# RWKV-7 and MLA trunk layer on one core: a new order for the first FFN's start, for the small RWKV weights and for the first chunk of head group 1

## The chip, the cores and the metric

One core of a Trainium2 chip runs the whole layer. The metric is device time in microseconds (us) of one execution, taken as the median of three runs. Traces come from one further, profiled execution.

## The reference, cut to what matters

T = 256 tokens, width 2048, FFN width 5504, one layer, all in f32.

```
x += 0.5 * post(FFN1(pre(x)))                 FFN = (silu(h @ w_gate) * (h @ w_up)) @ w_down
x += post((g_A * MLA(h) + g_B * RWKV7(h)) @ w_o),   h = pre(x)
x += post(XAttn(pre(x), mem))                 256 memory tokens, 4 heads
x += 0.5 * post(FFN2(pre(x)))

RWKV7, 16 heads of 64, per token t and head:
  w, a, g    from low-rank products (tanh(dw) @ w_w2, da @ w_a2, sigmoid(dg) @ w_g2)
  sa = S a_t;   S = S * w_t + sa (kk*a)_t + v_t k_t;   o_t = S r_t
  o = group_norm(o) * lnx_w + lnx_b + bonus;   y = (o * g) @ w_ob
```

pre and post are RMS norms; g_A and g_B are sigmoids of h times a gate weight of 2 x 2048 columns.

## The kernel before, in words

**Products.** Every weight is split into a high part that the TensorE's fast f32 mode keeps exactly (`whi`) and the rest (`wlo`), and every activation too (`hT` holds both). A weight tile of 128x1024 goes by the SP queue into one of four `wraw` buffers (L177), ACT casts it to `whi` (L179), DVE subtracts to get `wlo` (L180); three such pairs of slots exist. `lin_ch` makes outputs with channels on partitions: per k two matmuls for each 128 columns, L201 with `whi` (512 wide, both parts of the activation) and L204 with `wlo` (256 wide). `lin_tok` makes outputs with tokens on partitions: three matmuls of 512 (L222, L223, L224) per k and token half, and these three are called a step here; a gate chunk of 512 columns has 32 steps. `weights` issues the loads and splits ahead of use, so DVE and ACT do splits among their other work, each engine in one fixed order.

**Order.** A scheduler orders every engine's instructions by a priority that the program sets (`priority`, `hot`, `ahead`), and `after` adds a dependency by hand. On the chip each engine runs its list in order.

**First FFN.** x comes transposed (xT), times the norm's gain, straight into `hT` in pieces (`feed`), and the norm's row of 1/rms is applied to the products afterwards: the sums of squares come from x itself (`X`, four loads of 512 KB), `rstd` is finished by POOL's pow, and `row` spreads it over the partitions with two matmuls (`rB`, L264). The first gate and up columns (c0 = 0) are run in turns of four k.

**RWKV part.** Heads come in two groups of eight (g = 0, 1). `rw_prep` makes the low-rank products from the small weights `ww` (w_w2 and w_a2, matmul `lora`, L727), decay scans and so on; `rw_gram` makes 32x32 blocks of products per chunk of 32 tokens in `G`; `rw_inverse` writes the blocks to DRAM, inverts them row by row on DVE (`TT`, `tm`), writes the result to DRAM (`td`) and loads it back into `G` with four loads. `rw_chain` then runs eight chunks in sequence: `pu` (L875, needs `G`), the copy `uv` on DVE (L876), `pn` (L880) and `po`. After a chunk POOL's queue writes the output (`osc`). `rw_group_norm` loads them again (`ov`), normalises on DVE with a pow on POOL (`gv`), multiplies by g (`pg`) and transposes into `zh` and `zl` for w_ob.

Because chain and inverse leave TensorE idle, matmuls of other products fill it: the first product of the mixers' output (`out_a`, w_oa) and the eight gate chunks (`gate`, steps of three matmuls, called gates 0 to 7 here), whose results go to `ya` or by POOL's queue to `t1d`.

Of the kernel before, what the change touches and what calls it, by code (L numbers as in the profile page):

```python
# [10 lines left out]
F32 = mybir.dt.float32  # L11
# [3 lines left out]
ALU = mybir.AluOpType  # L15
# [12 lines left out]
RING = 3  # L28
STILL = (64, 32)
SKEW = 4  # L30
LEAD = 100
# [46 lines left out]
class Layer:  # L78
    def __init__(self, ctx, tc, a):
# [112 lines left out]

    def lin_ch_steps(self, w, nk, c0, n, x, evac, feed=None):

        nc = self.nc
        nt = n // P
        ps = [self.psm.tile([P, 2, T], F32, tag="mm", name="mm") for _ in range(nt)]
        for k, hi, lo in self.weights(w, nk, c0, n, feed, True):
            for j in range(nt):
                s = slice(j * P, (j + 1) * P)  # L200
                both = lambda: nc.tensor.matmul(ps[j], hi[:, s], x[:, k], start=(k == 0), stop=(k == nk - 1))  # L201
                if k < nk - 1:
                    both()
                nc.tensor.matmul(ps[j][:, 0, :], lo[:, s], x[:, k, 0], start=False, stop=False)  # L204
                if k == nk - 1:
                    both()
            yield k
        for j in range(nt):
            y = self.tmp.tile([P, T], F32, tag="half", name="half", bufs=2)
            nc.scalar.copy(out=y, in_=ps[j][:, 1, :])  # L210
            nc.vector.tensor_add(y, y, ps[j][:, 0, :])  # L211
            evac(j, y)

    def lin_tok(self, w, nk, c0, n, xh, xl, evac, skew=0):
# [5 lines left out]
        def step(t, k, hi, lo):  # L220
            s = slice(t * P, (t + 1) * P)
            nc.tensor.matmul(ps[t], xh[:, k, s], hi, start=(k == 0), stop=False)  # L222
            nc.tensor.matmul(ps[t], xh[:, k, s], lo, start=False, stop=False)  # L223
# [34 lines left out]

    def row(self, r):

        nc = self.nc
        ps = self.pss.tile([P, T], F32, tag="sm", name="rB")
        for t in range(NT):
            nc.tensor.matmul(  # L264
                ps[:, t * P : (t + 1) * P], r[t].broadcast_to([P, P]), self.ident, start=True, stop=True)
        out = self.stat.tile([P, T], F32, tag="row", name="row", bufs=2)
        nc.scalar.copy(out=out, in_=ps)
        return out

    def lazy_row(self, r):  # L270
        made = []

        def get():
            if not made:
                made.append(self.row(r() if callable(r) else r))
            return made[0]

        return get
# [64 lines left out]
    def pre_norm_input(self, srcT, gain, pool):  # L343
# [61 lines left out]
    def ffn(self, normed, wg, wu, wd, post):  # L405
        nc = self.nc
        h, _, row, *feed = normed
        with self.tc.tile_pool(name="hid", bufs=1) as hid:
            mh = hid.tile([P, KF, T], F32R, tag="mh", name="mh")
            ml = hid.tile([P, KF, T], F32R, tag="ml", name="ml")  # L410
            for c0 in range(0, DFF, 256):
                n = min(256, DFF - c0)
                gate = {}
# [12 lines left out]

                if c0 == 0:
                    both = (self.lin_ch_steps(wg, KD, c0, n, h, ev_gate, *feed),
                            self.lin_ch_steps(wu, KD, c0, n, h, ev_up))
                    for k in range(0, KD + 4, 4):  # L430
                        for steps in both:
                            for _ in zip(range(4), steps):
                                pass
                    continue
                self.lin_ch(wg, KD, c0, n, h, ev_gate)
                self.lin_ch(wu, KD, c0, n, h, ev_up)
            return self.post_norm(
# [263 lines left out]
    def rw_alloc(self, pool):  # L701
        self.pad(pool, 32)
        self.ar = pool.tile([P, NC, GP, P], F32, tag="ar", name="ar")
        self.bk = pool.tile([P, NC, GP, P], F32, tag="bk", name="bk")
        self.uv = pool.tile([P, NC, GP, 64], F32, tag="uv", name="uv")
        self.osc = self.dram.tile([T, 1024], F32, name="osc")
        self.nc.gpsimd.memset(self.ar, 0.0)

    def rw_prep(self, pool, g, r, k, bon):
        nc, a = self.nc, self.a  # L710
        p4 = lambda nm: pool.tile([P, GP, T], F32, tag="p4", name=nm, bufs=6)
        ww = pool.tile([P, 512], F32, tag="ww", name="ww")
        cs = slice(g * 512, (g + 1) * 512)
        nc.gpsimd.dma_start(out=ww[:64], in_=a["w_w2"][:, cs])
        nc.gpsimd.dma_start(out=ww[64:], in_=a["w_a2"][:, cs])
        for h in range(2):
# [109 lines left out]
    def rw_inverse(self, pool, G):  # L826
# [26 lines left out]
        for b in range(0, nb, nb // 2):  # L853
            for h in range(2):
                q = slice(h * C, (h + 1) * C)
                bs = slice(b, b + nb // 2)
                nc.sync.dma_start(out=gv[q, bs, q], in_=td[h, bs].rearrange("b s t -> s b t"))

    def rw_chain(self, pool, g, G, wc):
        nc = self.nc  # L860
        S = None
        for c in range(NC):
# [11 lines left out]
            for p in range(GP):  # L874
                nc.tensor.matmul(pu[:, p, :], G[:64, c, p, :64], rhs[:, p, :], start=True, stop=True)  # L875
            nc.vector.tensor_copy(out=self.uv[:64, c], in_=pu)  # L876
# [81 lines left out]
    def mix(self, normed, xsp, stop=None):  # L958
# [3 lines left out]
        with tc.tile_pool(name="mixp", bufs=1) as mp:  # L962
# [15 lines left out]
            with tc.tile_pool(name="rwkv", bufs=1) as pool:  # L978
# [8 lines left out]
                for g in range(2):  # L987
# [5 lines left out]
                    with self.hot():  # L993
                        self.rw_gram(G)
                        self.rw_inverse(pool, G)
                        self.rw_chain(pool, g, G, wc)
                    last_o.append(self.last_o)
                with self.priority(B + 10000):
                    for c in range(8):
                        s = slice(c % 4 * 512, (c % 4 + 1) * 512)  # L1000

                        def use0(t, x):
                            nc.vector.scalar_tensor_tensor(
                                out=ya[:, t, s], in0=x, scalar=1.0, in1=ya[:, t, s], op0=ALU.add, op1=ALU.mult)

                        def use1(t, x):
                            nc.gpsimd.dma_start(out=t1d[t * P : (t + 1) * P, s], in_=x)

                        self.gate(mp, normed, c, use0 if c < 4 else use1)
                tc.cur_priority = E  # L1010
# [115 lines left out]
def layer(ctx: ExitStack, tc, a, stop=None):  # L1126
    L = Layer(ctx, tc, a)

    def block(t, c):
        if c % 2 == 0:  # L1130
            s = slice(c * 512, (c + 2) * 512)
            load = tc.nc.sync.dma_start(out=L.X[:, t, s], in_=a["x"][t * P : (t + 1) * P, s])
            L.after(load, L.last_split)
        return L.X[:, t, c * 512 : (c + 1) * 512]

    h, feed = L.pre_norm_input(a["xT"], "n_ffn1_pre", L.hpool)
    normed = (h, *L.input_stats(block), feed)
    update = L.ffn(normed, a["w_ffn1_gate"], a["w_ffn1_up"], a["w_ffn1_down"], a["n_ffn1_post"])
# [85 lines left out]
```

## Time and profile before

| | |
|---|---|
| median of three runs | 2405.56 us (2404.24 to 2406.37) |
| profiled execution | 2409.81 us, span 2408.0 us, granted clock 0.993 |
| PE, DVE, ACT, POOL busy | 98%, 62%, 48%, 4% of the span |
| DMA | 450 MB, mean 187 GB/s |
| first FFN starts its matmuls at | 4.54 us |
| inverse, group 0 / group 1, ends | 1062.2 / 1233.6 us |
| chain, group 0 / group 1, first pu | 1071.8 / 1244.95 us |

A row of a timeline has start, duration, engine, line, operation, output<-inputs, shape and count, and in brackets the idle time before it with what ended it. A row of a window has the stretch, its length, the busy time (with count) of PE, weight load, DVE, ACT and POOL, the granted TensorE clock (1.00 is full), the DMA engines' busy share and GB/s. A row of waits names the waiting instruction, the one waited for, and total, number and longest of the waits in us. SPq and POOLq are the DMA queues of these engines.

### The profile page before, as it was taken

Reading aid. Unit: us, or ns where it says so; the run is one execution under the profiler, and the core shown is the slowest. Engines: PE = TensorE matmul, PEld = TensorE weight load, DVE = VectorE, ACT = ScalarE, POOL = GpSimd, SP = SyncE. Lnnn points to the kernel's source line nnn. Section 1 sums busy time; section 2 is a strip of 40 time slices with the busy share of each in tenths; the row PEclk is TensorE's granted clock in tenths of the full one; section 3 lists DMA queues with packets and bytes.
Section 4 is the critical chain, followed back from the end, with each engine's and each line's share of the span. In section 5 each row is a group of like instructions: output and inputs, shape, how many; then the busy total and the mean of one; then the engine's idle time right before and its main releaser. Section 6 shows DMA issues by size and latency. Waiting matters only on the chain.

```text
span 2408.0 us, 33178 instructions
## 1 busy us (share of the span) xinstructions
PE 2353.1 (98%) x12666; PEld 2005.5 (83%) x12666; DVE 1487.1 (62%) x2262; ACT 1145.0 (48%) x1703; POOL 87.8 (4%) x132
## 2 busy tenths in 40 slices
PE   8999999999999999999999999999999999999997
PEld 6888888888887887888877688987888888888886
DVE  5666666654447576785874756556766666664444
ACT  6544444444346555443433446545645444544443
POOL 0000000000000102002012100000000000000000
PEclk9999999999999999999999999999999999999999
DMA  7555555556666654463664666545555555566654
GB/s 253 188 191 193 188 189 192 190 191 195 198 199 198 214 175 132 148 190 109 191 196 137 235 230 206 171 155 167 185 192 191 188 190 193 188 198 195 201 194 144
DMA packets 138719, 450.23 MB, mean 187 GB/s; under 512 B 24000, under 2 KB 26560, under 8 KB 138304
## 3 DMA queue, kind: packets, MB, share of 16 engines
q1 hardware_dynamic: 132896, 434.17, 55.8%
q0 software_dynamic: 4944, 13.64, 1.9%
q8 instruction: 99, 1.62, 0.3%
q10 hardware_dynamic: 720, 0.30, 0.1%
q14 instruction: 60, 0.49, 0.1%
HBM read 437.56 MB, written 10.49 MB: 186 GB/s over the span
## 4 chain that ended last, share of the span: by engine, by line
PE 91%; DVE 3%; DMA 3%; issue 2%; ACT 1%; POOL 1%; SPq 0%; DVEq 0%; POOLq 0%; ACTq 0%
PE mm L201 31%; PE mm L204 16%; PE mm L223 13%; PE mm L224 13%; PE mm L222 13%; DVE wlo L180 1%; PE gr L821 1%; DVE X L400 1%; PE pn L880 1%; ACT whi L179 1%; PE po L866 1%; DMA ov<-osc 0%; PE po L889 0%; PE po L868 0%; PE pu L875 0%
## 5 line engine op out<-in xcount | busy, mean ns | idle before, releaser
L180 DVE TENSOR_TENSOR wlo<-wraw,whi 128x1024 fp32r<-128x1024 f32 (+2 forms) x796 | 958.2, 1206 | 709.2 <-ACT whi L179 696.9
L179 ACT CAST whi<-wraw 128x1024 fp32r<-128x1024 f32 (+2 forms) x796 | 824.0, 1037 | 895.3 <-PE mm L224 470.2
L201 PE MATMUL mm<-hT,whi 128*128 128x512 f32 x3296 | 1147.9, 394 | 6.6 <-DVE hT L292 5.4
L204 PE MATMUL mm<-hT,wlo 128*128 128x256 f32 x3296 | 913.5, 283 | 2.1 <-DVE wlo L180 2.1
L201 PEld LDWEIGHTS mm<-hT,whi 128*128 128x128 f32 x3296 | 614.1, 188 | 134.3 <-ACT whi L179 6.9
L204 PEld LDWEIGHTS mm<-hT,wlo 128*128 128x128 f32 x3296 | 621.5, 189 | 13.1 <-DVE wlo L180 4.1
L222 PE MATMUL mm<-whi,mh 128*128 128x512 f32 x688 | 267.6, 389 | 1.2 <-ACT whi L179 1.2
L223 PE MATMUL mm<-wlo,mh 128*128 128x512 f32 x688 | 267.8, 389 | 0.5 <-DVE wlo L180 0.5
L224 PE MATMUL mm<-whi,ml 128*128 128x512 f32 x688 | 267.7, 389 | 0.0
L223 PE MATMUL mm<-wlo,hT 128*128 128x512 f32 (+2 forms) x512 | 189.0, 369 | 3.5 <-DVE wlo L180 3.4
L222 PE MATMUL mm<-whi,hT 128*128 128x512 f32 (+2 forms) x512 | 187.1, 367 | 2.0 <-ACT whi L179 1.6
L224 PE MATMUL mm<-whi,hT 128*128 128x512 f32 (+2 forms) x512 | 187.8, 367 | 0.0
L222 PEld LDWEIGHTS mm<-whi,mh 128*128 128x128 f32 x688 | 129.1, 188 | 28.1 <-ACT whi L179 1.5
L223 PEld LDWEIGHTS mm<-wlo,mh 128*128 128x128 f32 x688 | 129.1, 188 | 27.7 <-DVE wlo L180 1.0
L224 PEld LDWEIGHTS mm<-whi,ml 128*128 128x128 f32 x688 | 129.2, 188 | 26.9
L210 ACT COPY half<-mm 128x256 f32<-128x256 f32 x206 | 75.1, 366 | 136.8 <-PE mm L201 136.8
L211 DVE TENSOR_TENSOR half<-half,mm 128x256 f32<-128x256 f32 x206 | 85.7, 418 | 53.0 <-ACT half L210 53.0
L223 PEld LDWEIGHTS mm<-wlo,hT 128*128 128x128 f32 x512 | 97.9, 191 | 19.8 <-DVE wlo L180 5.7
L222 PEld LDWEIGHTS mm<-whi,hT 128*128 128x128 f32 x512 | 97.8, 192 | 16.4 <-ACT whi L179 2.3
L224 PEld LDWEIGHTS mm<-whi,hT 128*128 128x128 f32 x512 | 97.9, 191 | 13.7 <-issue 0.2
L256 POOL TENSOR_TENSOR rstd<-rstd,mhalf 128x1 f32<-128x1 f32 x22 | 12.1, 553 | 1809.8 <-DVE rstd L254 1809.8
L222 PE MATMUL mm<-whi,oT 128*128 128x512 f32 x128 | 51.1, 401 | 1.4 <-ACT whi L179 1.4
(279 smaller groups left out, 1857.6 us busy)
## 6 DMA issues: line engine op xcount, KB each, us to landing
wraw<-in_w_ffn_up SPq DMA_DIRECT2D x172, 512.0 KB, 3.3
wraw<-in_w_ffn_gate SPq DMA_DIRECT2D x171, 512.0 KB, 3.3
wraw<-in_w_ffn_down SPq DMA_DIRECT2D x168, 512.0 KB, 4.2
wraw<-in_w_in SPq DMA_DIRECT2D x124, 512.0 KB, 3.5
wraw<-in_w_o SPq DMA_DIRECT2D x32, 512.0 KB, 4.3
wraw<-in_w_ckv SPq DMA_DIRECT2D x31, 512.0 KB, 3.5
wraw<-in_w_oa SPq DMA_DIRECT2D x16, 512.0 KB, 3.4
wraw<-in_w_ob SPq DMA_DIRECT2D x16, 512.0 KB, 4.8
```

Source lines behind the costliest of these rows:

```text
L179: cast = nc.scalar.copy(out=hi[:, e], in_=raw[:, e])
L180: self.last_split = nc.vector.tensor_sub(out=lo[:, e], in0=raw[:, e], in1=hi[:, e].bitcast(F32))
L201: both = lambda: nc.tensor.matmul(ps[j], hi[:, s], x[:, k], start=(k == 0), stop=(k == nk - 1))
L204: nc.tensor.matmul(ps[j][:, 0, :], lo[:, s], x[:, k, 0], start=False, stop=False)
L210: nc.scalar.copy(out=y, in_=ps[j][:, 1, :])
L211: nc.vector.tensor_add(y, y, ps[j][:, 0, :])
L222: nc.tensor.matmul(ps[t], xh[:, k, s], hi, start=(k == 0), stop=False)
L223: nc.tensor.matmul(ps[t], xh[:, k, s], lo, start=False, stop=False)
L224: self.last_mm = nc.tensor.matmul(ps[t], xl[:, k, s], hi, start=False, stop=(k == nk - 1))
L400: return nc.vector.scalar_tensor_tensor(out=x, in0=y[:, t, s], scalar=r[t], in1=x, op0=ALU.mult, op1=ALU.add)
L821: nc.tensor.matmul(ps[:, p, :], self.bk[:, c, p, :], self.ar[:, c, p, :], start=True, stop=True)
L866: nc.tensor.matmul(po[:, p, :], self.ar[:, c, p, :], S[:, p, :], start=(p == 0), stop=False)
```

## The change

Five edits:

- In the first FFN the four k of an xT tile share one `wraw` buffer (`self.xraw`); each of the four loads of x is issued after one four-k turn's split, in place of all four after the turns; the second gate chunk (c0 = 256) is run right behind them, into PSUM buffers of the tag "tr" (`spare`), and `rB` is tied behind its last matmul (`last_ch`).
- `rw_small` makes `ww` the first tile of the RWKV pool, with its loads ahead of the memset of `ar`.
- The gates are written ahead of group 1's chain.
- Group 1's first `pu` is tied behind the last matmul of gate step 210 (`filler[FIRST_U]`).
- The four loads of `G` go in turn to SP and POOL.

```diff
+FIRST_U = 209
...
-    def lin_ch_steps(self, w, nk, c0, n, x, evac, feed=None):
+    def lin_ch_steps(self, w, nk, c0, n, x, evac, feed=None, spare=False):
-        ps = [self.psm.tile([P, 2, T], F32, tag="mm", name="mm") for _ in range(nt)]
+        pool, tag = (self.pst, "tr") if spare else (self.psm, "mm")
+        ps = [pool.tile([P, 2, T], F32, tag=tag, name="mm") for _ in range(nt)]
...
-                    both()
+                    self.last_ch = both()
...
             self.last_mm = nc.tensor.matmul(ps[t], xl[:, k, s], hi, start=False, stop=(k == nk - 1))
+            self.filler.append(self.last_mm)
...
-    def row(self, r):
+    def row(self, r, prev=None):
...
+            if prev is not None:
+                self.after(one, prev)
...
-                made.append(self.row(r() if callable(r) else r))
+                made.append(self.row(r(), self.last_ch) if callable(r) else self.row(r))
...
         def feed(k0, m):
-            raw = self.wraw.tile([P, 4, T], F32, tag="wraw", name="wraw")
-            nc.sync.dma_start(out=raw[:, :m, :], in_=srcT[:, k0 : k0 + m, :])
+            if k0 % 4 == 0:
+                self.xraw = self.wraw.tile([P, 4, T], F32, tag="wraw", name="wraw")
+            raw = self.xraw[:, k0 % 4 : k0 % 4 + m, :]
+            nc.sync.dma_start(out=raw, in_=srcT[:, k0 : k0 + m, :])
...
+                both = (self.lin_ch_steps(wg, KD, c0, n, h, ev_gate, *feed[:1]),
+                        self.lin_ch_steps(wu, KD, c0, n, h, ev_up))
+                for k in range(0, KD, 4):
+                    for steps in both:
+                        for _ in zip(range(4), steps):
+                            pass
+                    if feed:
+                        feed[1](k // 4)
+                if feed:
+                    ev_gate, ev_up = evacs(256)
+                    third = self.lin_ch_steps(wg, KD, 256, n, h, ev_gate, spare=True)
+                    for _ in zip(range(KD), third):
+                        pass
+                    both = (*both, third)
...
     def rw_alloc(self, pool):
         self.pad(pool, 32)
+        self.rw_small(pool, 0)
...
+    def rw_small(self, pool, g):
+
+        self.ww = pool.tile([P, 512], F32, tag="ww", name="ww")
+        for q, n in ((slice(0, 64), "w_w2"), (slice(64, P), "w_a2")):
+            self.nc.gpsimd.dma_start(out=self.ww[q], in_=self.a[n][:, g * 512 : (g + 1) * 512])
...
-                nc.sync.dma_start(out=gv[q, bs, q], in_=td[h, bs].rearrange("b s t -> s b t"))
+                queue = (nc.sync, nc.gpsimd)[h]
+                queue.dma_start(out=gv[q, bs, q], in_=td[h, bs].rearrange("b s t -> s b t"))
...
+                if c == 0 and behind is not None:
+                    self.after(one, behind)
...
+                    if g == 1:
+                        self.filler = []
+                        with self.priority(B + 10000):
+                            for c in range(8):
...
+                                self.gate(mp, normed, c, use0 if c < 4 else use1)
+                    with self.hot():
+                        self.rw_chain(pool, g, G, wc, self.filler[FIRST_U] if g == 1 else None)
...
+    def load(i):
+        t, s = i // 2, slice(i % 2 * 1024, (i % 2 + 1) * 1024)
+        L.after(tc.nc.sync.dma_start(out=L.X[:, t, s], in_=a["x"][t * P : (t + 1) * P, s]), L.last_split)
```

What the instruction lists show at three places (numbers behind names are buffer numbers; the lines of the changed program differ from those of the profile: L204 and L208 there are L201 and L204 before, L226 to L228 are L222 to L224, L182 is L180, L912 is L875, L915 is L876, L919 is L880).

TensorE in the first FFN, before: the two matmuls of rB inside the second gate chunk (mm_398 and mm_399), the first of them at this place.

```order
L204 MATMUL mm_399<-hT_108,wlo_106 128x256
L201 MATMUL mm_398<-hT_108,whi_104 128x512
L204 MATMUL mm_398<-hT_108,wlo_106 128x256
L201 MATMUL mm_399<-hT_108,whi_104 128x512
L264 MATMUL rB_371<-ident_90,rstd_360 128x128
L204 MATMUL mm_399<-hT_108,wlo_106 128x256
L201 MATMUL mm_398<-hT_108,whi_104 128x512
```

TensorE in the first FFN, after: the end of the second gate chunk (mm_334 and mm_335), rB, and the second up chunk (mm_491 and mm_492).

```order
L204 MATMUL mm_334<-hT_108,whi_104 128x512
L208 MATMUL mm_335<-hT_108,wlo_106 128x256
L204 MATMUL mm_335<-hT_108,whi_104 128x512
L269 MATMUL rB_450<-ident_90,rstd_439 128x128
L269 MATMUL rB_450<-ident_90,rstd_445 128x128
L204 MATMUL mm_491<-hT_108,whi_104 128x512
L208 MATMUL mm_491<-hT_108,wlo_106 128x256
```

rB has moved from inside that chunk to behind its 32 pairs.

TensorE at the start of the RWKV part, before: the last matmuls of the k columns (mm_7698), then sixteen of w_oa (mm_7804 and mm_7805), of which the last five are shown, then lora.

```order
L224 MATMUL mm_7805<-whi_104,oT_7108 128x512
L222 MATMUL mm_7804<-whi_104,oT_7108 128x512
L223 MATMUL mm_7804<-wlo_106,oT_7108 128x512
L224 MATMUL mm_7804<-whi_104,oT_7108 128x512
L222 MATMUL mm_7805<-whi_104,oT_7108 128x512
L727 MATMUL lora_8086<-twa_6274,ww_8077 128x512
L727 MATMUL lora_8090<-twa_6274,ww_8077 128x512
```

After, at the same place:

```order
L204 MATMUL mm_7695<-hT_5731,whi_104 128x512
L226 MATMUL mm_7804<-whi_104,oT_7105 128x512
L226 MATMUL mm_7805<-whi_104,oT_7105 128x512
L762 MATMUL lora_8083<-twa_6271,ww_7796 128x512
L762 MATMUL lora_8087<-twa_6271,ww_7796 128x512
L227 MATMUL mm_7804<-wlo_106,oT_7105 128x512
```

lora has moved ahead of fourteen matmuls of w_oa; on POOL the two loads of ww now stand ahead of the memset of ar instead of behind it.

DVE around the first uv of group 1, before (wlo by the tile of its wraw: 10456 holds k = 6 and 7 of gate 6, 10472 k = 8 and 9).

```order
L919 TENSOR_REDUCE gm_10723<-ov_10719 128x8
L929 TENSOR_TENSOR ov_10691<-ov_10691,gv_10696 128x512
L180 TENSOR_TENSOR wlo_106<-wraw_10456,whi_104 128x1024
L930 TENSOR_TENSOR ov_10691<-ov_10691,lnx_10688 128x512
L920 TENSOR_SCALAR gm_10723<-gm_10723 128x8
L927 TENSOR_TENSOR ov_10719<-ov_10719,bon_7797 128x512
L931 TENSOR_TENSOR ov_10691<-ov_10691 128x512
L180 TENSOR_TENSOR wlo_106<-wraw_10472,whi_104 128x1024
L921 TENSOR_TENSOR ov_10719<-ov_10719,gm_10723 128x512
L876 COPY uv_7801<-pu_9328 64x256
```

After (wraw_10210 holds k = 6 and 7, 10226 k = 8 and 9); the first reduce, of ov_10716, stands eight rows ahead of the first row shown, the low of 10210 six and that of 10226 one.

```order
L969 TENSOR_TENSOR ov_10688<-ov_10688,lnx_10685 128x512
L962 TENSOR_REDUCE gv_10721<-gsc_10719 128x8
L182 TENSOR_TENSOR wlo_106<-wraw_10242,whi_104 128x1024
L970 TENSOR_TENSOR ov_10688<-ov_10688 128x512
L963 TENSOR_SCALAR gv_10721<-gv_10721 128x8
L968 TENSOR_TENSOR ov_10716<-ov_10716,gv_10721 128x512
L182 TENSOR_TENSOR wlo_106<-wraw_10258,whi_104 128x1024
L915 COPY uv_7801<-pu_10445 64x256
```

Between the group norm's first reduce and uv there now stand four lows instead of two, and a product with gv, which POOL's pow makes. On TensorE the first pu stood behind 11 steps and one matmul of gate 6, and now stands behind 18 steps, twenty matmuls later; five matmuls stand between pu and pn in both.

More of the change, by code (lines that the diff above doesn't have):

```diff
@@ L200, in lin_ch_steps @@
                 s = slice(j * P, (j + 1) * P)
-                both = lambda: nc.tensor.matmul(ps[j], hi[:, s], x[:, k], start=(k == 0), stop=(k == nk - 1))
+                both = lambda: nc.tensor.matmul(
+                    ps[j], hi[:, s], x[:, k], start=(k == 0), stop=(k == nk - 1))
                 if k < nk - 1:
@@ L263, in row @@
         for t in range(NT):
-            nc.tensor.matmul(
+            one = nc.tensor.matmul(
                 ps[:, t * P : (t + 1) * P], r[t].broadcast_to([P, P]), self.ident, start=True, stop=True)
+            if prev is not None:
+                self.after(one, prev)
         out = self.stat.tile([P, T], F32, tag="row", name="row", bufs=2)
@@ L410, in ffn, with evacs @@
             ml = hid.tile([P, KF, T], F32R, tag="ml", name="ml")
-            for c0 in range(0, DFF, 256):
-                n = min(256, DFF - c0)
+            def evacs(c0):
                 gate = {}
@@ L425, in ev_up @@
                     self.split(gate[j], mh[:, k, :], ml[:, k, :])
[L427 to L433, printed above, removed]
-                    continue
-                self.lin_ch(wg, KD, c0, n, h, ev_gate)
-                self.lin_ch(wu, KD, c0, n, h, ev_up)
+                return ev_gate, ev_up
+            for c0 in range(0, DFF, 256):
+                n = min(256, DFF - c0)
+                if feed and c0 == 256:
+                    continue
+                ev_gate, ev_up = evacs(c0)
+                if c0:
+                    self.lin_ch(wg, KD, c0, n, h, ev_gate)
+                    self.lin_ch(wu, KD, c0, n, h, ev_up)
+                    continue
+                both = (self.lin_ch_steps(wg, KD, c0, n, h, ev_gate, *feed[:1]),
[12 more added lines that the diff above has]
+                    both = (*both, third)
+                for steps in both:
+                    for _ in steps:
+                        pass
+                if feed:
+                    self.lin_ch(wu, KD, 256, n, h, ev_up)
             return self.post_norm(
@@ L711, in rw_prep @@
         p4 = lambda nm: pool.tile([P, GP, T], F32, tag="p4", name=nm, bufs=6)
[L712 to L715, printed above, removed]
+        if g:
+            self.rw_small(pool, g)
+        ww = self.ww
         for h in range(2):
@@ L874, in rw_chain @@
             for p in range(GP):
-                nc.tensor.matmul(pu[:, p, :], G[:64, c, p, :64], rhs[:, p, :], start=True, stop=True)
+                one = nc.tensor.matmul(pu[:, p, :], G[:64, c, p, :64], rhs[:, p, :], start=True, stop=True)
+                if c == 0 and behind is not None:
+                    self.after(one, behind)
             nc.vector.tensor_copy(out=self.uv[:64, c], in_=pu)
@@ L995, in mix, with use0, use1 @@
                         self.rw_inverse(pool, G)
-                        self.rw_chain(pool, g, G, wc)
-                    last_o.append(self.last_o)
[L998 to L1009, printed above, removed]
+                    if g == 1:
+                        self.filler = []
+                        with self.priority(B + 10000):
+                            for c in range(8):
+                                s = slice(c % 4 * 512, (c % 4 + 1) * 512)
+                                def use0(t, x):
+                                    nc.vector.scalar_tensor_tensor(
+                                        out=ya[:, t, s], in0=x, scalar=1.0, in1=ya[:, t, s], op0=ALU.add, op1=ALU.mult)
+                                def use1(t, x):
+                                    nc.gpsimd.dma_start(out=t1d[t * P : (t + 1) * P, s], in_=x)
+                                self.gate(mp, normed, c, use0 if c < 4 else use1)
+                    with self.hot():
+                        self.rw_chain(pool, g, G, wc, self.filler[FIRST_U] if g == 1 else None)
+                    last_o.append(self.last_o)
                 tc.cur_priority = E
@@ L1127, in layer @@
     L = Layer(ctx, tc, a)
+    def load(i):
+        t, s = i // 2, slice(i % 2 * 1024, (i % 2 + 1) * 1024)
+        L.after(tc.nc.sync.dma_start(out=L.X[:, t, s], in_=a["x"][t * P : (t + 1) * P, s]), L.last_split)
     def block(t, c):
[L1130 to L1133, printed above, removed]
         return L.X[:, t, c * 512 : (c + 1) * 512]
     h, feed = L.pre_norm_input(a["xT"], "n_ffn1_pre", L.hpool)
-    normed = (h, *L.input_stats(block), feed)
+    normed = (h, *L.input_stats(block), feed, load)
     update = L.ffn(normed, a["w_ffn1_gate"], a["w_ffn1_up"], a["w_ffn1_down"], a["n_ffn1_post"])
```

2 lines of the change are left out of this document (1 added, 1 removed).

## The prediction

> **What bounds the kernel now.** I read the page's first lines, then ten-microsecond windows of the start and the middle, then the TensorE's waits there and, around each, the timeline of the engine that is waited for.
>
> ```profile
> span 2408.0 us, 33178 instructions
> PE 2353.1 (98%) x12666; PEld 2005.5 (83%) x12666; DVE 1487.1 (62%) x2262; ACT 1145.0 (48%) x1703; POOL 87.8 (4%) x132
> ```
>
> TensorE is busy in 98% of the span, and the change takes no sizeable work from it. What can be won lies in the 55 us in which it isn't busy and in the stretches where its clock is lower. The parts of the change aim at three of these stretches: the first 50 us, the start of the RWKV part at 935 to 945, and the first chunk of head group 1 at 1241 to 1257.
>
> ```profile
> 10.00:20.00 10.00, 7.79 (x40) 5.93 (x40) 6.89 (x12) 7.39 (x12) 0.00 (x0) 1.00 0.90 289
> 20.00:30.00 10.00, 10.00 (x59) 8.72 (x59) 7.13 (x9) 5.91 (x9) 0.00 (x0) 1.00 0.88 290
> 30.00:40.00 10.00, 6.35 (x37) 5.32 (x35) 4.10 (x8) 6.45 (x15) 0.55 (x1) 1.00 0.94 351
> 40.00:50.00 10.00, 10.00 (x50) 8.82 (x51) 6.01 (x14) 7.77 (x16) 0.55 (x1) 0.83 0.55 193
> ...
> 940.00:950.00 10.00, 7.60 (x26) 4.38 (x25) 1.92 (x2) 6.56 (x14) 3.45 (x4) 1.00 0.71 202
> 1245.00:1302.00 57.00, 55.59 (x389) 45.70 (x390) 26.31 (x43) 15.55 (x26) 9.85 (x17) 0.91 0.35 109
> ```
>
> The columns are busy time of PE, weight load, DVE, ACT and POOL, then the granted clock, the DMA share and GB/s. Between 30 and 40 us TensorE stands for 3.65 us, and from 40 to 50 the clock is 0.83.
>
> **Part 1, the first FFN's start.**
>
> ```profile
> 28.41 1.83 SPq L1132 DMA_DIRECT2D X<-in_x  x4
> 34.90 0.63 ACT L283 ACTIVATE junk<-X 128x512 f32<-128x512 f32 x1 [3.42 <-DMA X<-in_x]
> 40.98 0.63 ACT L283 ACTIVATE junk<-X 128x512 f32<-128x512 f32 x1
> 39.90 0.49 PE L264 MATMUL rB<-ident,rstd 128*128 128x128 f32 x2 [3.65 <-POOL rstd L256]
> 42.76 0.63 PE L201 MATMUL mm<-hT,whi 128*128 128x512 f32 x1
> 43.40 0.63 PE L201 MATMUL mm<-hT,whi 128*128 128x512 f32 x1
> 45.97 0.39 PE L201 MATMUL mm<-hT,whi 128*128 128x512 f32 x1
> 46.32 0.40 PE L201 MATMUL mm<-hT,whi 128*128 128x512 f32 x1
> X<-in_x SPq DMA_DIRECT2D x4, 512.0 KB, 7.7
> ```
>
> The four x pieces go out only at 28.41, each takes 7.7 us to land, the eight sums of squares run from 34.90 to 41.6, and the broadcast of rstd (rB), which stands inside the second gate chunk, makes TensorE wait 3.65 us. After it five pairs come 0.64 us apart instead of 0.35: 5 x 0.29 = 1.45 us. The new order sends one x piece after each four-k stage and puts the whole second gate chunk ahead of rB: 32 pairs x 0.35 = 11.2 us. The last x piece stands behind that chunk's second weight tile on SP; landing (7.7), two sums of squares (1.5) and the rstd steps (about 2) are 11.2 us from its issue, and the issue comes some microseconds before that chunk begins, so I expect no wait at rB: 3.65 + 1.45 = 5.1 us won.
>
> Against it: the x pieces now travel in the four stages in which the DMAs already carry 289 GB/s at a share of 0.90. Three pieces of 512 KB at the 351 GB/s of the third window cost 4.5 us of transfer; the idle tenth of three stages of 5.6 us (16 pairs) holds 1.9, so up to 2.6 us may appear as waits. In return the first xT pieces no longer take a weight buffer each, and up to the 2.2 us that TensorE misses between 10 and 20 can be had. I take these two against each other: -5 us, with ends -7.3 (5.1 + 2.2) and -2.5 (5.1 - 2.6).
>
> The second gate chunk accumulates in the PSUM buffers of the transposes ("tr"), which nothing else uses in this stretch: 0. The shared xT buffer serves the memory's first pieces in the cross-attention too.
>
> ```profile
> PE mm L204 <- DVE wlo L180: 1.0, 2, 0.6
> ```
>
> That is the largest kind of wait where these pieces are read (1456 to 1490 us); with one buffer less in use it can shrink, with a longer hold of that one grow: 0, ends -1 and +1.
>
> **Part 2, small weights first.**
>
> ```profile
> PE lora L727 <- DMA ww<-in_w_a: 2.4, 1, 2.4
> PE rnb L768 <- DVE bych L760: 0.8, 1, 0.8
> PE mm L223 <- DVE wlo L180: 0.6, 1, 0.6
> 933.72 3.52 POOL L707 MEMSET ar<- 128x4096 f32 x1 [81.81 <-PE po L609]
> 937.18 0.55 POOL L714 DMA_DIRECT2D ww<-in_w_w  x1
> 937.72 0.53 POOL L715 DMA_DIRECT2D ww<-in_w_a  x1
> 936.18 0.73 PE L222 MATMUL mm<-whi,oT 128*128 128x512 f32 x2 [1.41 <-ACT whi L179]
> 943.36 1.96 PE L727 MATMUL lora<-twa,ww 128*128 128x512 f32 x4 [2.40 <-DMA ww<-in_w_a]
> ```
>
> On POOL the 3.52 us memset stood ahead of ww's two loads; lora starts 5.6 us after the second is issued. With the loads first they go out at 933.72 and 934.3, and ww is there at about 939.9. But lora moves too: before it stood behind 16 matmuls of the w_oa column, now behind two, which TensorE ends at 936.9. So the 2.4 us aren't removed; TensorE stands about 3 us at lora instead, and only the 0.6 us for wlo and the 0.8 at rnb go. I take -1 us: (2.4 + 0.6 + 0.8) - 3.0 = 0.8. Ends: -3.2 if ww is there as lora comes, +2 if that wait, right behind the 1.41 us one, lowers the clock as the 3.65 us one did. This is where the Trainium skill's page "TensorE: Matmul & The Clock Gate", section "What's actually happening", bears: an idle window of about 3.4 us that runs freely throttles the clock, so two near waits can count as one. By it this term would be at its upper end. The trace agrees for 3.65 us, and 940 to 950 with one wait of 2.40 stayed at 1.00.
>
> **Part 3, group 1's first u (pu) and the inverse.**
>
> ```profile
> 1233.37 0.21 DVE L851 TENSOR_TENSOR TT<-TT,tm 64x31 f32<-64x31 f32 x1
> 1234.65 0.54 POOL L912 DMA_DIRECT2D ov<-osc  x1
> 1236.88 4.75 SPq L857 DMA_DIRECT2D G<-td  x4
> 1240.96 0.39 PE L222 MATMUL mm<-whi,hT 128*128 128x512 f32 x1
> 1241.64 0.39 PE L222 MATMUL mm<-whi,hT 128*128 128x512 f32 x1
> 1244.95 0.65 PE L875 MATMUL pu<-rhs,G 64*64 64x64 f32 x8 [2.92 <-DMA G<-td]
> 1248.94 1.97 PE L880 MATMUL pn<-uv,bk 128*128 128x64 f32 x8 [1.41 <-DVE uv L876]
> 1242.52 0.69 DVE L919 TENSOR_REDUCE gm<-ov 128x8 f32<-128x512 f32 x1 [4.68 <-DMA ov<-osc]
> 1243.72 1.22 DVE L180 TENSOR_TENSOR wlo<-wraw,whi 128x1024 fp32r<-128x1024 f32 x1
> 1248.48 0.41 DVE L876 COPY uv<-pu 64x256 f32<-64x256 f32 x1
> 1252.00 0.17 DVE L924 TENSOR_SCALAR gv<-gv 128x8 f32<-128x8 f32 x1
> 1255.43 0.69 DVE L929 TENSOR_TENSOR ov<-ov,gv 128x512 f32<-128x512 f32 x1 [3.26 <-POOL gv L926]
> ```
>
> The inverse ends at 1233.6, G is back at 1244.95, and TensorE, out of work at 1241.9, waits 2.92 us, then 1.41 more at pn for the copy uv; the clock is 0.91 over the chain. Now 20 more matmuls stand ahead of pu: 20 x 0.227 = 4.5 us of cover (two L222 rows with two matmuls between them start 0.68 us apart, so 0.227 each), and two of the four G loads go out on POOL. SP needs 4.75 us for the four issues, so halves could save up to 2.4 us, but the 4.5 us of cover already exceed the 2.92. I cost the second queue at 0, here and in group 0. The Trainium skill's page "DMA: Bandwidth & Descriptors", section "Issuing engines are not separate DMA queues", says as much: a second issuer saves only issue time. No row shows otherwise.
>
> What decides is DVE, which works in order. It stood from 1237.8 to 1242.52 for the group norm's ov<-osc, which POOL issues one microsecond after the inverse and which takes 7.9 us. In the new order the lows (wlo) of gate 6's k = 6 and k = 8 stand behind that wait and are now needed ahead of pu, and uv stands behind more: before, uv came 6.0 us behind the landing; now between them also stand a third and fourth wlo (1.2 us each) and ov<-ov,gv, which waits for POOL's pow (3.26 us above, some 2 without the DMA issues that delayed it). Step by step, with the inverse's end kept at 1233.6: TensorE needs k = 6's low at 1242.5 and has it at 1244.9 (the 1243.72 row's end): 2.4 us of wait. The low of k = 8 comes at 1248.0 against 1247.7: 0.3. pu runs at 1249.1, and with five matmuls behind it TensorE is at pn at 1250.9. DVE: from 1248.0 an ov, a reduce, a wlo, an ov and gv (3.0 us), pow to 1253.0, ov, wlo and uv (2.2): 1255.2. So pn starts at 1255.2 instead of 1248.94: 6.2 us later, 4.5 of them work done earlier, +1.7 us. The matmuls behind pn then run as slowly as before. I take +1.7: it rests on rows of this stretch and on the order; ends -8.3 (both waits, 4.3, and some 4 us of the lower clock) and +4.
>
> **Part 4, the end of group 1.**
>
> ```profile
> 1320.94 0.59 POOL L912 DMA_DIRECT2D ov<-osc  x1
> 1326.49 0.69 DVE L919 TENSOR_REDUCE gm<-ov 128x8 f32<-128x512 f32 x1 [2.20 <-DMA ov<-osc]
> ```
>
> The second token half's ov load stood behind the first half's pow on POOL; now it stands ahead of it and can go out some 5 us sooner. But 14 matmuls fewer are left to cover the tail (14 x 0.227 = 3.2 us). I take -1, ends -4 and +3.
>
> **Sum.** -5 - 1 + 1.7 - 1 = -5.3. The profiled execution took 2409.81 us, its span plus 1.8, and would be 2404.5; the median of the runs lies 4.25 below it, so 2400.3. Differences under 0.2% (4.8 us) can't be told from none here; this forecast lies just outside.
>
> **Rivals.**
> First: group 1's waits go. If the ov load lands before DVE gets to it, or DVE reaches uv by 1250, the waits and the low clock go: -6 instead of +1.7, in all -13, 2392.6. For it speaks that G has 1.6 us to spare; against it, the 4.68 us row.
> Second, slower: x pieces in the early stages. ACT takes their sums of squares in order ahead of the next stage's highs, so a piece that lands 7.7 us after its issue can hold a stage of 5.6 us by 2.1 us. Three stages make 6.3, and eight pairs each at the slow 0.64 make 3 x 2.3 = 6.9 more; less the 5.1 won, +8.1, with the other terms +7.8: 2413. It decides from 1.7 us a stage on (5.1 / 3). Against it: the pieces are issued a stage ahead, and the low clock has to come three times.
> Third: the stages lose just what rB gives (2.6 us, and 2 us more at rB because the last piece is late), the start wins 0.5, and all stays within 0.2%: about 2405.
>
> **How the numbers follow.** Chances: forecast 0.45 (2396 to 2405 by its ends), first rival 0.25, second 0.12, third 0.18. Faster by over 0.2% is below 2400.75: all of the first rival and about six in ten of the forecast, 0.53. Slower is the second and the worst of the others, 0.14; the rest is 0.33. The range goes from the first rival's far side, 2391, to the second's near side, 2409.
>
> **What would show it.** Part 1 is right if no wait at rB over 0.5 us is left and the clock of 40 to 50 is 1.00; wrong if the windows up to 30 lose more than 2 us against these. Part 2: a wait at lora of 2 to 3 us now at 937. Part 3: no wait for G, one for wlo near k = 6 and one at pn of about 4 us; if these two are missing, the first rival holds. Part 4: the second ov<-osc issued before the first pow.

## The result, and the profile after

The change made the kernel slower: 2412.99 us median of nine runs (2406.78 to 2421.16) against 2404.24 for the kernel before in the same nine rounds, a ratio of 1.0037 with a 95% interval of 1.0024 to 1.0050, so some 9 us (6 to 12). I had forecast 2400.3. Single executions of one kernel scatter more than the parts of this change weigh: the kernel before ran between 2399 and 2411 us over all experiments. The profiled execution of the changed kernel took 2421.16 us, the slowest of its nine.

The first lines of the page after, to be held against those of before:

```profile
span 2419.4 us, 33174 instructions
PE 2364.2 (98%) x12666; PEld 2013.6 (83%) x12666; DVE 1486.5 (61%) x2262; ACT 1144.7 (47%) x1703; POOL 90.4 (4%) x136
```

The span is 11.4 us longer, and TensorE is busy 11.1 us more with the same 12666 matmuls. The idle time is 55 us in both, so the waits have only moved, and the 11 us have gone into a lower clock. Windows of after:

```profile
10.00:20.00 10.00, 7.95 (x36) 6.41 (x35) 6.39 (x11) 7.85 (x16) 0.00 (x0) 0.83 0.82 301
20.00:30.00 10.00, 9.40 (x53) 7.71 (x52) 6.68 (x13) 6.91 (x12) 0.55 (x1) 1.00 0.80 282
30.00:40.00 10.00, 9.26 (x54) 7.88 (x54) 5.56 (x10) 7.48 (x14) 0.56 (x1) 1.00 0.97 343
40.00:50.00 10.00, 10.00 (x61) 8.86 (x60) 5.32 (x6) 4.92 (x6) 0.00 (x0) 1.00 0.73 241
...
1070.00:1080.00 10.00, 8.66 (x48) 7.59 (x48) 1.97 (x3) 0.58 (x2) 1.02 (x2) 0.66 0.50 165
...
1260.00:1270.00 10.00, 10.00 (x45) 8.09 (x45) 2.15 (x4) 1.78 (x3) 1.06 (x2) 0.50 0.31 103
1270.00:1280.00 10.00, 10.00 (x56) 8.35 (x55) 2.49 (x4) 1.78 (x3) 0.98 (x2) 0.69 0.18 59
```

The start is a little better: rB waits for nothing, and 30 to 50 us holds 115 matmuls in place of 87, though 10 to 30 holds 89 in place of 99. The two losses are at 1070 and from 1250 on. The timeline at group 0's first pu, TensorE and then the issues on SP and POOL:

```profile
1068.74 0.39 PE L228 MATMUL mm<-whi,hT 128*128 128x512 f32 x1
1071.34 1.07 PE L912 MATMUL pu<-rhs,G 64*64 64x64 f32 x8 [2.21 <-DMA G<-td]
...
1061.38 0.47 SPq L887 DMA_DIRECT2D td<-TT  x1
1066.65 0.86 SPq L893 DMA_DIRECT2D G<-td  x2
...
1067.16 1.34 POOL L893 DMA_DIRECT2D G<-td  x2 [78.76 <-DMA wraw<-in_w_in]
```

Before, pu stood at 1071.78 with no wait, 9.5 us behind the inverse's end (1062.24). Now TensorE comes to it at 1069.13, 8.0 us behind that end (1061.11), waits 2.21 us and runs at a clock of 0.66 behind it. Two things have moved. pu stands seven matmuls, or 1.5 us, sooner in TensorE's list. And the load that it waits for, the second of the four, comes 2.0 us later: on SP it landed 7.9 us behind td's issue (1062.52 to 1070.41), 1.4 us ahead of pu; on POOL it lands 9.9 us behind it (1061.38 to 1071.29). The loads of G in group 0 with the median time from issue to landing, before (first row) and after:

```profile
G<-td SPq DMA_DIRECT2D x4, 64.0 KB, 2.3
...
G<-td SPq DMA_DIRECT2D x2, 64.0 KB, 2.5
G<-td POOLq DMA_DIRECT2D x2, 64.0 KB, 4.7
```

Group 1, TensorE and then DVE:

```profile
1248.89 0.50 PE L227 MATMUL mm<-wlo,hT 128*128 128x512 f32 x1 [1.90 <-DVE wlo L182]
1253.26 0.68 PE L912 MATMUL pu<-rhs,G 64*64 64x64 f32 x8
1258.82 1.70 PE L919 MATMUL pn<-uv,bk 128*128 128x64 f32 x8 [3.51 <-DVE uv L915]
1277.49 0.50 PE L226 MATMUL mm<-whi,hT 128*128 128x512 f32 x1
...
1246.41 0.69 DVE L958 TENSOR_REDUCE gm<-ov 128x8 f32<-128x512 f32 x1 [3.91 <-DMA ov<-osc]
1256.61 0.69 DVE L968 TENSOR_TENSOR ov<-ov,gv 128x512 f32<-128x512 f32 x1 [1.75 <-POOL gv L965]
1258.35 0.41 DVE L915 COPY uv<-pu 64x256 f32<-64x256 f32 x1
```

The wait for G is gone, as the tie was to do. In its place stand 1.90 us for the low of k = 6 and 3.51 us for uv, which DVE makes 11.9 us behind the start of the group norm's reduce. The low clock that follows lasts from 1259 to 1276, some 17 us, where before it lasted from 1246 to 1256.

### The profile page after: what moved, and what is told of

It is laid out like the page before. It is cut to its first block, busy times and chain, and to the rows that moved or that the text cites. A ratio compares the mean times of both kernels' runs of the same rounds, so it can differ in the third digit from the quotient of the medians.

```text
span 2419.4 us, 33174 instructions
## 1 busy us (share of the span) xinstructions
PE 2364.2 (98%) x12666; PEld 2013.6 (83%) x12666; DVE 1486.5 (61%) x2262; ACT 1144.7 (47%) x1703; POOL 90.4 (4%) x136
## 4 chain that ended last, share of the span: by engine, by line
PE 89%; DVE 4%; DMA 3%; issue 2%; ACT 1%; POOL 1%; SPq 0%; DVEq 0%; POOLq 0%; ACTq 0%
PE mm L204 30%; PE mm L208 15%; PE mm L228 13%; PE mm L227 13%; PE mm L226 12%; DVE wlo L182 2%; PE gr L856 1%; PE pn L919 1%; PE po L903 1%; DVE X L409 1%; ACT whi L181 1%; PE po L928 0%; PE po L905 0%; PE pu L912 0%; PE lora L762 0%
## 5 line engine op out<-in xcount | busy, mean ns | idle before, releaser
L182 DVE TENSOR_TENSOR wlo<-wraw,whi 128x1024 fp32r<-128x1024 f32 (+2 forms) x796 | 958.4, 1206 | 709.6 <-ACT whi L181 697.2
L204 PE MATMUL mm<-hT,whi 128*128 128x512 f32 x3296 | 1147.1, 394 | 7.0 <-DVE hT L299 5.4
L208 PE MATMUL mm<-hT,wlo 128*128 128x256 f32 x3296 | 912.6, 282 | 2.0 <-DVE wlo L182 2.0
L204 PEld LDWEIGHTS mm<-hT,whi 128*128 128x128 f32 x3296 | 613.7, 188 | 134.7 <-ACT whi L181 7.3
L208 PEld LDWEIGHTS mm<-hT,wlo 128*128 128x128 f32 x3296 | 621.3, 189 | 12.9 <-DVE wlo L182 3.9
L226 PE MATMUL mm<-whi,mh 128*128 128x512 f32 x688 | 268.3, 390 | 1.2 <-ACT whi L181 1.2
L228 PE MATMUL mm<-whi,ml 128*128 128x512 f32 x688 | 268.3, 390 | 0.0
L226 PE MATMUL mm<-whi,hT 128*128 128x512 f32 (+2 forms) x512 | 188.4, 369 | 2.4 <-ACT whi L181 2.0
L228 PE MATMUL mm<-whi,hT 128*128 128x512 f32 (+2 forms) x512 | 189.1, 370 | 0.0
L226 PEld LDWEIGHTS mm<-whi,mh 128*128 128x128 f32 x688 | 129.4, 188 | 28.3 <-ACT whi L181 1.5
L228 PEld LDWEIGHTS mm<-whi,ml 128*128 128x128 f32 x688 | 129.5, 188 | 26.9
L226 PEld LDWEIGHTS mm<-whi,hT 128*128 128x128 f32 x512 | 98.4, 193 | 16.9 <-ACT whi L181 2.7
L228 PEld LDWEIGHTS mm<-whi,hT 128*128 128x128 f32 x512 | 98.5, 192 | 14.1 <-issue 0.2
L226 PE MATMUL mm<-whi,oT 128*128 128x512 f32 x128 | 50.6, 396 | 1.4 <-ACT whi L181 1.4
```

What stands on the lines that cost most here:

```text
L182: self.last_split = nc.vector.tensor_sub(out=lo[:, e], in0=raw[:, e], in1=hi[:, e].bitcast(F32))
```

## The experiments

Each figure in us below is the ratio to the runs of the kernel before on the same chip, with its 95% interval, times 2404.5. Theory: the loss has two sources, the second queue (through the place of pu) and the tie (through DVE's order). Rival: the parts work as they were priced, and something else, such as the start's DMA load, costs.

**One part alone, four times.** Each kernel has one edit of the change and is the kernel before in all else.

```diff
e1_start:  +  the three streams, load(i) between them, last_ch, xraw
e2_ww:     +        self.rw_small(pool, 0)          # ahead of ar and its memset
e3_tie:    +                        self.rw_chain(pool, g, G, wc, self.filler[FIRST_U] if g == 1 else None)
e4_queue:  +                queue = (nc.sync, nc.gpsimd)[h]
```

> The first FFN's part alone (shared xT buffer, x loads between the stages, the second gate chunk ahead of rB); all else as before. Theory A (the gain at rB is given back in the stages: slow clock and waits between 10 and 40 us): 1 to 2 us faster than before, no wait at rB, clock of 10 to 20 us below 1.00. Theory B (the start wins 5 us as I predicted and another part hides it): 4 to 6 us faster.

Measured: 0.9983 (0.9974 to 0.9992), 4.1 us faster (1.9 to 6.3). TensorE's windows and waits in this kernel:

```profile
20.00:30.00 10.00, 8.52 (x44) 6.33 (x43) 7.19 (x13) 6.93 (x12) 0.55 (x1) 1.00 0.84 276
...
PE mm L208 <- DVE wlo L182: 2.8, 5, 0.8
```

No wait at rB is left, and the stages lose some of it: five short waits for lows, 2.8 us in all, where before had two of 1.0. The start doesn't cost, so the rival named above falls for it. The ratio is about what I had put, and neither theory's figure is excluded. The traces put the start itself lower: the first 300 matmuls take 60.9 us here and 63.7 and 61.0 in two profiles of the kernel before; over all profiles they take 62.0 on average with the old start (eight, 60.6 to 64.5) and 61.1 with the new (six, 60.5 to 61.9). In this profile 2.6 us of the gain lie in group 1's chain and tail (116.5 us between the same two matmuls, 119.1 before), which the edit doesn't touch.

> The small weights' part alone. Theory A (the wait at lora moves and gets shorter, 1.2 us instead of 2.4, and the one at rnb goes from 0.8 to 0.2): 1 to 2 us faster. Theory B (the time won is waited again at group 0's first pu, because G does not come earlier): no change within 1 us, with a new wait for G of 0.5 to 2 us near 1070.

Measured: 0.9991 (0.9980 to 1.0002), 2.2 us faster, an interval that just reaches no change. The waits at lora and rnb in its profile are 1.2 and 0.2, and group 0's first pu waits for nothing, as theory A has it. The wait at lora tells little: in kernels without this edit it is 1.2 to 1.5 in four profiles, 2.4 in two and absent in two. The one at rnb tells more: 0.8 in all eight profiles without the edit and 0.2 in all six with it. The 500 matmuls around it take 106.7 to 108.0 us with the edit and 108.1 to 110.7 without, 1.4 us less on average.

> The tie of group 1's first pu behind 210 gate steps alone (with the gates written ahead of the chain). Theory A (DVE reaches the lows of k = 6 and uv only behind the group norm's wait for its ov load): 2 to 6 us slower; no wait for G, about 2 us at the low of k = 6, 3.5 to 4.5 us at pn, and the clock at half for some 10 us behind it. Theory B (the tie does what it says): the wait for G and the low clock go, 4 to 6 us faster.

Measured: 1.0022 (1.0013 to 1.0031), 5.3 us slower (3 to 7). Its waits from 1240 to 1330:

```profile
PE pn L895 <- DVE uv L891: 3.7, 1, 3.7
...
PE mm L227 <- DVE wlo L182: 1.8, 1, 1.8
```

No wait for G, and the two waits that DVE's order forecast. Theory B falls. pn starts 20.6 us behind the inverse's end, 5.2 later than before, and 4.5 of these are work done earlier, so little is lost there; and the clock behind it is at half from 1250.9 to 1257.7 only, 6.8 us, where before had 10.2. More is lost in the tail behind the chain. Its windows, before (first row) and in this kernel:

```profile
1320.00:1330.00 10.00, 7.33 (x31) 4.82 (x31) 7.80 (x14) 3.32 (x5) 3.16 (x5) 1.00 0.75 269
...
1320.00:1330.00 10.00, 9.76 (x30) 6.82 (x30) 6.76 (x12) 1.64 (x2) 2.88 (x4) 0.70 0.47 160
```

All six profiles of kernels with the tie have the clock at half for some 6.8 us in the tail; of the other eight, seven have 1.00 throughout and e4_queue 0.83 for ten microseconds. From the same matmul ahead of group 1's chain to the same one behind its tail, this kernel takes 123.2 us and e9_no_queue 123.0; the five profiles with neither tie nor second queue take 116.1 to 119.2.

> The inverse's write-back on two queues alone. Theory A (the scheduler, which reckons two queues as quicker, puts group 0's first pu 7 rows earlier on TensorE, but G does not land earlier): 2 to 5 us slower, a wait for G of 1 to 2.5 us near 1071 with a lower clock behind it. Theory B (as I predicted, the second queue costs and brings nothing in group 0): within 1 us; in group 1 the wait for G gets shorter by 1 to 2.4 us, then 1 to 2 us faster.

Measured: 1.0038 (1.0024 to 1.0053), 9.1 us slower (6 to 13): the larger of the two losses, and more than theory A's 2 to 5. Waits from 1060 to 1130 and from 1240 to 1330, and three windows:

```profile
PE pu L888 <- DMA G<-td: 1.7, 1, 1.7
...
PE tr L308 <- DVE ov L949: 4.0, 1, 4.0
PE pu L888 <- DMA G<-td: 3.7, 1, 3.7
...
1070.00:1080.00 10.00, 10.00 (x80) 8.52 (x81) 5.48 (x9) 2.82 (x6) 1.01 (x2) 1.00 0.40 129
1240.00:1250.00 10.00, 6.32 (x31) 5.29 (x30) 6.70 (x11) 1.59 (x2) 1.03 (x1) 0.68 0.82 262
1250.00:1260.00 10.00, 10.00 (x39) 7.94 (x39) 3.34 (x7) 1.78 (x3) 2.72 (x3) 0.50 0.17 61
```

The instruction lists show one reason why both waits for G grew. In the kernel before, group 0's first pu stands at row 5384 of TensorE's list and group 1's at row 6016 (a run of equal rows counted once); with the second queue they stand at 5377 and 6009, though nothing ties them. Seven matmuls less, 1.6 us of cover, are ahead of each pu. The other reason is that G comes no sooner, and in group 0 later. There the loads that pu needs have landed 7.1 to 8.1 us behind td's issue with SP alone (nine profiles) and 8.0 to 10.2 with two queues (five); in group 1 it is 10.5 to 11.7 and 10.4 to 11.5. The lists of DVE and ACT changed too, and the longest wait is one of 4.0 us in the tail, with the clock at 0.83 from 1320 to 1330.

**The second queue with pu kept in its place.** The gates are written ahead of both chains, and both groups' first pu are tied to the matmul behind which they stood before; with this and SP alone the lists of all engines are those of before. Then one group only is held.

```diff
+FIRST_U = (90, 609)        # e5_queue_order; e10_queue_g0: (47, 609), which leaves group 0's pu at row 5377
...
+            self.filler.append(nc.tensor.matmul(ps[t], xh[:, k, s], hi, start=(k == 0), stop=False))
+                        self.rw_chain(pool, g, G, wc, self.filler[FIRST_U[g]])
```

> The inverse's write-back on two queues, but both groups' first pu tied to the TensorE row at which they stand in the kernel before (behind 91 and 610 gate matmuls; with the second queue alone they stood 7 rows earlier). Theory A (the second queue cost 9 us by the earlier place of pu, through the waits for G and the low clock behind them): the loss goes, within 2 us of before, no wait for G in group 0 and at most 3 us in group 1. Theory B (loads of G on POOL's queue land later or hold POOL up): still 5 us slower or more.

Measured: 1.0011 (1.0002 to 1.0021), 2.6 us slower (0.5 to 5). No wait for G in group 0; in group 1:

```profile
PE pu L888 <- DMA G<-td: 3.2, 1, 3.2
...
1250.00:1260.00 10.00, 10.00 (x73) 8.07 (x72) 5.45 (x8) 3.19 (x5) 1.87 (x3) 1.00 0.27 90
```

Holding the two places takes away some 6.5 of the 9.1 us. That doesn't rule out theory B's later landing: in group 0 G is late here too (8.8 us behind td's issue), and the old place of pu covers it by 0.5 us. In group 1 a wait of 3.2 us stays, as the second queue brings G no sooner. What the 2.6 us are is open; with two queues DVE's list still differs from that of before in 17 rows around group 1's first uv, and pn stands two matmuls sooner.

> The second queue with group 1's first pu held at its old TensorE row, group 0's left 7 rows earlier. It splits the second queue's 9 us (2.6 us were left with both held). If group 0's wait carries it: 5 us or more slower than before; if group 1's wait and low clock do: 2 to 4 us slower, with a wait for G of 1 to 2.5 us in group 0 alone.

Measured: 1.0022 (1.0011 to 1.0033), 5.3 us slower (2.6 to 7.9). By difference group 0's earlier pu costs 2.7 us (5.3 less 2.6) and group 1's 3.8 (9.1 less 5.3), but neither difference is clear of none. In this kernel's profile the wait in group 0 was only 0.3 us, below what I expected; it varies from run to run. The traces price group 0 more sharply. From the end of its inverse to group 1's first lora TensorE has the same matmuls to do in every kernel: it takes 55.5 us in all ten profiles with pu in its old place, 56.0 here and 57.4 in e4_queue.

**The tie with uv first.** On DVE the group norm's reduce and its product with bon, both of group 0's second token half, are tied behind group 1's first uv, so that DVE doesn't stand for that half's load ahead of uv. No wait is taken away; other work comes first.

```diff
+            copied = nc.vector.tensor_copy(out=self.uv[:64, c], in_=pu)
+            if c == 0:
+                self.first_uv = copied
...
+            if (g, t) == (0, 1):
+                self.after(reduce, self.first_uv)
...
+            if (g, t) == (0, 1):
+                self.after(mul, self.first_uv)
```

> The tie of pu behind 210 gate steps alone, and in the group norm of group 0's second token half the first reduce and the product with bon tied on DVE behind group 1's first uv, so that nothing ahead of uv waits for that half's load. Theory A (that wait on DVE was what cost): no wait at the low of k = 6, none over 1 us at pn, clock 1.00, 3 to 6 us faster than before, 8 to 12 faster than the tie alone. Theory B (the later start of the chain costs, because 14 matmuls fewer cover the tail): 2 us slower to 2 us faster than before.

Measured: 0.9991 (0.9983 to 0.9999), 2.2 us faster than before (0.2 to 4.1), 7.5 us faster than the tie alone. The windows:

```profile
1240.00:1250.00 10.00, 10.00 (x72) 8.09 (x71) 6.76 (x12) 3.46 (x5) 1.06 (x2) 1.00 0.85 315
1250.00:1260.00 10.00, 10.00 (x76) 8.42 (x76) 6.36 (x11) 3.19 (x5) 2.72 (x3) 1.00 0.21 69
...
PE tr L308 <- DVE ov L955: 4.1, 2, 3.4
```

Every wait over 0.3 us at the start of group 1's chain is gone and the clock is full: the mechanism is shown. The gain is less than the 3 to 6 us expected. Part of the rest went into the tail, where theory B had its loss: the last row, from 1240 to 1330, shows a longer wait there (before: 2.2 between 1296 and 1350), 23 matmuls fewer are left to cover it, and the clock is 0.91 from 1300 to 1310 and 0.74 from 1310 to 1320, where before stayed at 1.00.

**Parts together.**

```diff
e7_all_uv:    the changed kernel, with
-                queue = (nc.sync, nc.gpsimd)[h]
+                queue = nc.sync
              and the ties of e6_tie_uv
e8_start_ww:  the changed kernel without tie and second queue
e9_no_queue:  the changed kernel without the second queue
```

> The changed kernel with the write-back on SP alone and the group norm's two instructions tied behind the first uv. If the parts add as they did alone: start 3 to 4 us, small weights 2, tie with uv first 3 to 6: 8 to 12 us faster than before. If the parts overlap (time won ahead of a chain is waited again at G): 3 to 6 us faster.

Measured: 0.9986 (0.9977 to 0.9995), 3.4 us faster than before (1.2 to 5.5), so it beats both kernels, but not the start alone (4.1), and it is less than the sum of its parts. Neither pu waits for G in its profile, so the time won isn't waited again there.

> The first FFN's start and the small weights together, tie and second queue undone. If they add: 5 to 6 us faster than before; if what both win is waited again at group 1's G: 2 to 3 us faster. The changed kernel less the two parts that cost; together with their 5 and 9 us alone it tells whether the whole is the sum.

Measured: 0.9988 (0.9979 to 0.9996), 2.9 us faster (1.0 to 5.0), again less than the 6.3 of the two alone; the intervals reach both. In its profile group 1's pu waits 2.8 us for G, as before (2.9 and 2.6), so the longer wait of the second theory isn't seen.

> The changed kernel with the write-back on SP alone; first FFN, small weights and tie stay. If the second queue is what makes it slower: 7 to 10 us below the changed kernel, within 2.5 us of before, with no wait at group 0's first pu and the waits at the low of k = 6 and at pn as in the tie alone. If the tie's loss decides: 3 to 6 us slower than before.

Measured: 1.0015 (1.0005 to 1.0025), 3.6 us slower (1.2 to 6.0). The second queue is 5.3 of the change's 8.9 us (8.9 less 3.6), which is what e10_queue_g0 gave with group 1's pu held, as the tie holds it here. The rest, 3.6, is what the tie costs (5.3) less what start and weights give back, 1.7. Between e6_tie_uv and e7_all_uv these two give 1.2, in e8_start_ww 2.9: all below the 6.3 of the two alone and around the 2.3 that the traces show in their own stretches (0.9 and 1.4). So the 4.1 of e1_start is probably too high. The four parts alone add up to 8.1 us slower, and the whole measured 8.9; that is close in part by luck, as the second queue cost 9.1 alone and 5.3 within the change.

**Second profiles.**

> The changed kernel once more, for a second profile, since its profiled execution was the slowest of its runs: if the waits in both groups are the cause, they are there again (G in group 0 1 to 2.5 us, low of k = 6 1.5 to 2.5, pn 3 to 4.5), and what differs between executions is the clock behind them.

One execution of 2415.89 us. Waits (group 0, then group 1) and windows:

```profile
PE pu L912 <- DMA G<-td: 2.5, 1, 2.5
...
PE pn L919 <- DVE uv L915: 2.2, 1, 2.2
PE mm L227 <- DVE wlo L182: 1.8, 1, 1.8
...
1070.00:1080.00 10.00, 10.00 (x45) 8.19 (x46) 1.55 (x3) 1.36 (x3) 1.02 (x2) 0.50 0.20 59
1080.00:1090.00 10.00, 10.00 (x49) 8.47 (x49) 5.12 (x8) 3.46 (x5) 0.99 (x2) 0.66 0.27 85
```

The same three waits, pn's shorter than expected. The clock behind group 0's wait fell to 0.50 and was still 0.66 from 1080 to 1090, where the first profile had 1.00 by then. From the end of group 0's inverse to group 1's first lora it takes 67.1 us here and 60.9 in the first profile, 11.6 and 5.4 more than with pu in its old place.

> The kernel before once more, for a second profile: its first one was 4 us above the median of its runs. If the sizes of the waits that I took from it were those of a slow execution, rB's wait is 2 to 3 us here and the low clock behind it and behind group 1's first pu is shorter; if not, they repeat within 0.3 us.

One execution of 2409.54 us.

```profile
PE rB L264 <- POOL rstd L256: 2.0, 1, 2.0
...
40.00:50.00 10.00, 10.00 (x60) 8.61 (x59) 8.14 (x16) 8.46 (x16) 0.56 (x1) 1.00 0.53 194
```

rB's wait is 2.0 here, not 3.65, and no low clock follows from 40 to 50. Over the eight profiles of kernels with the old start it lay between 1.5 and 3.7, and the clock from 40 to 50 was below 1.00 in four of them (0.73 to 0.92). The low clock at group 1 did come back (0.78 and 0.71 from 1240 to 1260), so that half of the expectation failed.

## Why the prediction was wrong

**The step that failed is "I cost the second queue at 0, here and in group 0"** (part 3). It measured 9.1 us alone and, by difference, 5.3 within the change. I had weighed issue time, and put at nothing, without a row, the two things that moved in group 0. One is the order: the first pu stands seven matmuls sooner in the changed kernel's list than in that of before, and I showed three places of the lists without that one. The other is the landing: the load that pu needs came 2.0 us later from POOL's queue. Before, G had 1.4 us to spare there. With the place held the later landing made no wait (e5_queue_order); the earlier place alone would have made about 0.1 us (1.5 less 1.4), which is an estimate, as no run has it with SP alone. Together they made the waits of 2.2 and 2.5 us and the low clock behind them. The sentence of the Trainium skill's page "DMA: Bandwidth & Descriptors", section "Issuing engines are not separate DMA queues", that a second issuer saves only issue time agrees with e5_queue_order as far as G came no sooner with the places held; I read it as "costs nothing", which it doesn't say.

**The tie: its waits right, its price wrong.** All the waits were where the prediction put them: 1.90 us at the low of k = 6 (2.4 forecast), 3.51 at pn (4.3), none for G. The net was put at +1.7, and the tie alone measured 5.3. Up to pn the sum was rather too high: in e3_tie 0.7 us are lost there. "The matmuls behind pn then run as slowly as before" was no worse: the low clock lasted 6.8 us in e3_tie and 10.2 before, though 17 in the first profile of the changed kernel. The term that was mis-sized is part 4, the tail, put at -1. I had counted the matmuls that no longer cover it and no clock. In the six profiles with the tie the longest wait in the tail is 1.9 to 3.4 us and the clock is at half for 6.8 us, which costs about half of that (an estimate); in the two of before the longest wait is 1.7 and the clock stays at 1.00. e6_tie_uv shows that DVE's order causes the two waits at the start of the chain, since they and the low clock behind them go with it; the loss in the tail stays there.

**The start.** -5 with ends -7.3 and -2.5; e1_start measured -4.1 (-6.3 to -1.9), and the traces show some 0.9 in the start itself. The 5.1 us at rB were near the upper end of what an execution shows: over eight profiles the wait is 2.6 us on average, with a low clock behind it in four. The stages up to 30 us gave up 10 matmuls, about 1.8 us at the 0.35 of a pair, just under the 2 us at which I would have called the part wrong. The rival by which x in the early stages slows the kernel didn't happen; that its number, 2413, is the one measured is luck.

**Small weights.** -1, measured -2.2 with an interval that holds both; the traces show 1.4 around lora. lora did move and wait again, 1.2 us instead of the 3.0 forecast: ww took 3.4 us from its second issue to lora, where I had carried over 5.6. The rows of after, POOL's and TensorE's:

```profile
935.06 0.52 POOL L743 DMA_DIRECT2D ww<-in_w_a  x1
...
938.43 3.58 PE L762 MATMUL lora<-twa,ww 128*128 128x512 f32 x4 [1.21 <-DMA ww<-in_w_a]
```

**The tail** (-1) had no experiment of its own; the windows with the tie show that it cost instead, but not how much of the 5.3 is its share. The first rival (2392.6) needed both group-1 waits gone, as in e6_tie_uv; even then it gave 2.2 us and not 6 to 8. I took the sizes of waits and low clock from one execution, 4 us above its median, and added them as if every run had them.

## What to carry to other kernels

Where a scheduler sets the order, an edit that looks local to a DMA queue can move compute: compare every engine's list at each place that waits for that transfer, and ask how much cover is left and when the data lands from the new queue. A tie that covers one wait helps only if whatever the tied work needs next isn't queued behind a wait on another in-order engine, and if the matmuls that it uses up aren't the cover of a later stretch; here two ties on DVE turned 5.3 us lost into 2.2 won. Prices of waits and of low clock taken from a single execution are samples: a second profile of the same kernel had one of them at little over half.

## What the runs showed of the hardware

A wait of some 2 us for G could cost far more than itself, and not by a fixed rule. In group 0 a wait of 2.21 us cost 5.4 us up to group 1's first lora, with the clock at half for 6.8 us; one of 2.47 us cost 11.6, with 20.5 us at half; and one of 1.75 us, in e4_queue, cost 1.9, with none. So what the wait costs is about itself and half the stretch of low clock. The same wait of 2.4 us at lora left the clock from 940 to 950 at 1.00 in one profile of before and at 0.83 in the other. The Trainium skill's page "TensorE: Matmul & The Clock Gate", section "What's actually happening", has a free-running idle window of about 3.4 us behind the throttle. That agrees with the luck in these, in that like waits have unlike ends, and with the lengths: all 74 stretches at half clock in the fourteen profiles last 3.4, 6.8, 10.2, 17.1 or 20.5 us. That waits of 2.2 and 2.5 us were enough is less than that page's figure, and in a chain of small matmuls the clock stayed low for up to 20.5 us, where the page has about 3.4 us of busy time to recover.

The same 64 KB loads of G took longer from POOL's queue in one place and not in the other: in group 0 a median of 4.7 us from issue to landing against 2.5 on SP in the changed kernel, in group 1 6.3 against 8.2. Why is open.
